# Seven products of a pair: three calls of 256 columns instead of one of 512 and one of 256, in three of fourteen pairs of a layer

## The chip, the core and the metric

One core of a Trainium2 chip runs the whole program in one launch. The metric is the device time of that launch in microseconds; the time of before is the median of three runs. One more execution was taken with the hardware profiler; all rows of the profile come from it.

## What is computed

A decoder trunk of two layers on one sequence of 512 tokens, 1024 wide, in 32-bit floats. Each layer has a mixer (windowed attention and retention behind one projection) and then an MLP with 4096 hidden columns. Only the MLP matters here:

```python
h2 = rmsnorm(x, g_mlp)
x = x + jnp.square(jax.nn.relu(h2 @ w_up)) @ w_down
```

## The kernel before

Every array lies with its features on the 128 partitions and the 512 tokens along the free dimension. To keep precision, each operand is split into a high and a low part (`hi` and `lo`); ACT copies the high part (L239), and DVE subtracts it from the value to give the low part (L240). A product of two such operands is three calls on TensorE: high by high, high by low, low by high (`products`, L284 to L286).

Weights come in units of 128 x 1024 floats. SP issues their loads (L183; for pairs L197, L199 and L202) into `raw` tiles, of which there are three; then follow the split on ACT and DVE into `hi` and `lo` tiles (three buffers each), and the calls on TensorE. `unit` takes the next unit and sees that the two behind it are being split already.

The MLP runs in the order of `mlp_sequence`. Its hidden columns are 32 chunks of 128. The first four go as one group ("first"); their results are scaled, cut at zero, squared and split by `put_up` (L1018, L1019, L291, L292). The other 28 go as 14 pairs of two neighbouring chunks, named here by the first of the two: 4, 6, 8, ... 30. Between the pairs stand the "down" steps (`two_chunks`), which multiply a quarter of the hidden columns into two chunks of the result. The two pairs 4 and 6 follow the first group directly; the last pair is 30; behind it the last quarter goes down, in layer 1 by `end`, which works on halves of 256 tokens and keeps the splits of its last five weight units in the tiles named `r`.

A pair is computed by seven products of half size instead of eight: the two chunks, the two halves of the input features and the two halves of the tokens (`H` = 256 each) make 2 x 2 blocks. The four parts of a pair (`order` entries with part 0 to 3) are weight blocks and sums of them, built on DVE (`add_part`, L208 to L216). `block` gives parts of the input, `form` sums of them (in r tiles). Each of the seven products runs over four slices of 128 features. Their accumulators are three PSUM banks, `a`, `e` and `b`; `b` starts as a copy of `a`, made by ACT (L1065), onto which TensorE goes on accumulating.

In each slice the high weights meet the high and the low part of the input in one call of 512 columns (L1041), and the low weights meet the high part in one of 256 (L1042). So each accumulator has two halves of 256 columns, and the halves have to be added afterwards: `join` (a copy of one half on ACT, L1047, and a sum on DVE, L1048), and `join_copied` (three sums on DVE, L1052 to L1054, with the copies `eu` and `bu` that ACT makes at L1067 and L1070). Then the result is scaled and cut at zero (L1085), squared (L1088) and split (L291, L292).

The order on each engine is fixed when the program is built, by a scheduler that places the instructions; engines wait for each other by semaphores. ACT, DVE and SP each work strictly through their own list. PSUM has five banks for such products (`ps_mm`).

Of the kernel before, what the change touches and what calls it, by code (L numbers as in the profile page):

```python
# [12 lines left out]
AF = mybir.ActivationFunctionType  # L13
ALU = mybir.AluOpType
# [3 lines left out]
P = 128  # L18
# [29 lines left out]
DEEP = 3  # L48
DELAY = 2
ASIDE = 48  # L50


def unit_order():
# [21 lines left out]
def mlp_sequence():  # L75

    seq = [("first", 0, 0), ("pair", 0, 2), ("pair", 0, 3)]
    for q in range(3):  # L80
        for i in range(4):
            seq += [("down", q, i), ("pair", q + 1, i)]
    return seq + [("last", 3, 0)]


class Slots:
# [29 lines left out]
def decoder(ctx, tc, xT, x_first, w_in, w_a, w_b, w_out, w_up, w_down, tables, decay, band, out):  # L116
    nc = tc.nc
    weights = {"w_in": w_in, "w_a": w_a, "w_b": w_b, "w_out": w_out, "w_up": w_up, "w_down": w_down}
# [6 lines left out]
    ps_mm = ctx.enter_context(tc.tile_pool(name="ps_mm", bufs=5, space=PSUM))  # L125
# [5 lines left out]
    def temp(name="t"):  # L131
        return tmp.tile([P, T], F32, tag="t", name=name)

    def big(name, dtype=F32):
        return tmp.tile([P, 2, T], dtype, tag="big", name=name, bufs=6)

    def bank(pool, name):
        return pool.tile([P, T], F32, tag=pool.name, name=name)
# [11 lines left out]
    xh, xl = xhl[:, 0], xhl[:, 1]  # L150
# [4 lines left out]
    order = [(layer, *u) for layer in range(DEPTH) for u in unit_order()]  # L155
# [62 lines left out]
    def split_until(n):  # L218
        while state["split"] < min(n, len(order)):
            i = state["split"]  # L220
            load_until(i + 3)
            paired = order[i][1] == "pair"
            if paired:
                add_part(i)
            raw = raws[i]
            if homes and i >= len(order) - len(homes):
                home = homes[len(order) - 1 - i]
                hi, lo = (home[:, 2 * a : 2 * a + 2, :].rearrange("p a t -> p (a t)") for a in range(2))
            else:

                first = (ASIDE, 0) if paired else (ASIDE, ASIDE) if i >= len(order) - 8 else (0, 0)
                hi, lo = (
                    wpool.tile([P, UNIT + P], F32R, tag=n, name=n)[:, a : a + UNIT] for n, a in zip(("hi", "lo"), first)
                )
            for at in (LEFT,) if paired and order[i][3] == 3 else halves(i):
                if i == 0 and at.start == 0:
                    nc.vector.tensor_copy(hi[:, at], raw[:, at])
                else:
                    nc.scalar.activation(hi[:, at], raw[:, at], AF.Copy)  # L239
                nc.vector.tensor_tensor(lo[:, at], raw[:, at], f32(hi[:, at]), ALU.subtract)  # L240
            raws.pop(i - 3 if paired else i, None)
            parts[i] = (hi, lo)
            state["split"] += 1

    def unit(name, layer):
        i = state["next"]
        assert order[i][:2] == (layer, name), (order[i], layer, name)
        state["next"] += 1
        split_until(i + 3)
        return parts.pop(i)  # L250
# [27 lines left out]
    def products(ps, pairs, start, stop, resume=False):  # L278


        n = len(pairs)
        for i, ((ah, al), (bh, bl)) in enumerate(pairs):
            more = {"skip_group_check": True} if resume else {}
            nc.tensor.matmul(ps, ah, bh, start=start and i == 0, stop=False, **more)  # L284
            nc.tensor.matmul(ps, ah, bl, start=False, stop=False, **more)  # L285
            nc.tensor.matmul(ps, al, bh, start=False, stop=stop and i == n - 1, **more)  # L286
# [197 lines left out]
    def layer_body(layer):  # L484
        g_mix, g_mlp = 2 * layer, 2 * layer + 1
        rms_mix, rms_mlp = Rms(g_mix), Rms(g_mlp)
# [410 lines left out]
        for u in range(4):  # L897
            hi, lo = unit("w_a", layer)
            for j in range(2):
                c = 2 * u + j  # L900
                ps = bank(ps_mm, "mm")
                pairs = []
# [76 lines left out]
        H = T // 2  # L979
# [26 lines left out]
        def form(j):  # L1006
            return [by_form[2 * (j // 2) + k // 2][:, j % 2, k % 2, :, :] for k in range(4)]

        def block(half, tokens):
            at = slice(tokens * H, tokens * H + H)  # L1010
            return [xhl[:, :, k, at] for k in range(4 * half, 4 * half + 4)]
# [13 lines left out]
        def up_home():  # L1025

            if any(len(f) == 4 for f in slots.free):
                t, own = slots.four()
                return t[:, 0:2, :], t[:, 2:4, :], own
            return big("uhi", F32R), big("ulo", F32R), []  # L1030

        def pair(q):
            def multiply(ps, weights, left, moving, start=True):


                hi, lo = weights
                more = {} if start else {"skip_group_check": True}
                both = ps.rearrange("p (s t) -> p s t", t=H)
                for k, m in enumerate(moving):
                    c = slice((0 if left else 4 * P) + k * P, (0 if left else 4 * P) + (k + 1) * P)  # L1040
                    nc.tensor.matmul(both, hi[:, c], m, start=start and k == 0, stop=False, **more)  # L1041
                    nc.tensor.matmul(ps[:, :H], lo[:, c], m[:, 0, :], start=False, stop=k == 3 and start, **more)  # L1042

            def join(dest, ps):

                side = temp("side")[:, :H]
                nc.scalar.activation(side, ps[:, H:], AF.Copy)  # L1047
                nc.vector.tensor_tensor(dest, ps[:, :H], side, ALU.add)  # L1048

            def join_copied(dest, ps, u):  # L1050

                nc.vector.tensor_tensor(u[:, :H], u[:, :H], u[:, H:], ALU.add)  # L1052
                nc.vector.tensor_tensor(u[:, :H], u[:, :H], ps[:, H:], ALU.add)
                nc.vector.tensor_tensor(dest, ps[:, :H], u[:, :H], ALU.add)  # L1054

            a, e, b = (bank(ps_mm, "mm") for _ in range(3))
            eu, bu, z = temp("eu"), temp("bu"), big("z")
            part = unit("pair", layer)
            multiply(a, part, True, block(0, 0))
            nc.scalar.activation(b, a, AF.Copy)  # L1065
            multiply(e, part, False, form(0))
            nc.scalar.activation(eu, e, AF.Copy)  # L1067
            part = unit("pair", layer)
            multiply(b, part, True, form(1), False)
            nc.scalar.activation(bu, b, AF.Copy)  # L1070
            multiply(a, part, False, block(1, 0), False)
            join(z[:, 0, :H], a)
            part = unit("pair", layer)
            multiply(b, part, True, form(2), False)
            join_copied(z[:, 1, H:], b, eu)
            multiply(e, part, False, block(1, 1), False)
            join_copied(z[:, 0, H:], e, bu)
            part = unit("pair", layer)
            multiply(b, part, True, form(3), False)
            for half in (1, 0):  # L1080
                at = slice(half * H, half * H + H)
                if half == 0:
                    join(z[:, 1, at], b)
                factor = rms_mlp.value[:, at].unsqueeze(1).broadcast_to([P, 2, H])
                nc.vector.scalar_tensor_tensor(z[:, :, at], z[:, :, at], 0.0, factor, ALU.max, ALU.mult)  # L1085
            hi, lo, own = up_home()
            for i in range(2):
                nc.scalar.activation(z[:, i, :], z[:, i, :], AF.Square)  # L1088
                split(hi[:, i, :], lo[:, i, :], z[:, i, :])
                up[q].append((hi[:, i, :], lo[:, i, :]))  # L1090
            up_slots[q].extend(own)
# [18 lines left out]
        for what, q, i in mlp_sequence():  # L1110
            if what == "first":
                group("w_up", layer, xs, [put_up] * 4, first_hooks())
            elif what == "pair":
                pair(q)
                if (q, i) == (3, 3):
                    for t in sums:
                        slots.give(*t[1])
            elif what == "down":
                two_chunks("w_down", layer, up[q], [put_down(2 * i), put_down(2 * i + 1)])
                if i == 3:  # L1120
                    slots.give(*up_slots[q])
            elif layer == DEPTH - 1:
                end(layer, up[q])
            else:
                group("w_down", layer, up[q], [put_down(c, True) for c in range(4)])
                for c in range(4, KD):
                    chunk("w_down", layer, up[q], put_down(c, True))
                slots.give(*up_slots[q])
# [156 lines left out]
```

## Time and profile before

| | us |
|---|---|
| median of 3 runs | 1505.27 |
| lowest and highest run | 1504.72, 1505.3 |
| profiled execution | 1504.95 |
| span of its trace | 1503.2 |
| TensorE busy in it | 1488.1 |
| DVE busy | 1076.2 |
| ACT busy | 763.3 |

In the rows shown below, PE is TensorE, PEld its loads of weights, and SPq the queue that SP issues to. A row of instructions in order of time has the start and the duration in us, the engine, the source line, the operation, the tiles (written <- read), the shape, how many there are, and in brackets how long the engine had been idle and what ended that. A tile's name is without its number, so that all `hi` tiles read alike; `mm` is an accumulator, `xhl` the split input of the layer, `r` a slot of the store for split activations and, in `end`, for weights, `uhi` and `ulo` split hidden columns outside that store. A row of a table by stretches has the stretch, its length, and each engine's busy time with the number of instructions, then the granted clock of TensorE, the share of the DMA engines and what they moved.

### The profile page before, as it was taken

The page shows a single profiled execution, that of the slowest core. Times are in us where ns is not written, and L with a number is a line of the kernel's source. Part 1 is how long each engine was busy: PE and PEld are TensorE (multiplying, and loading weights), DVE is VectorE, ACT ScalarE, POOL GpSimd, SP SyncE. Part 2 cuts the span into 40 slices and gives each one's busy share as a digit, 9 for nine tenths or more (in the row PEclk, how much of TensorE's full clock was granted, in tenths as well). Part 3 has the DMA queues.
Part 4 walks back from the last instruction along what each step waited for, and adds up shares of the span by engine and source line. Part 5 has one row for each costly group of instructions (what it writes and reads, how often), then busy time and mean ns, then how long its engine had stood idle before and what let it go on. Part 6 is the DMA issues. An engine that isn't in the chain of part 4 may idle for free.

```text
span 1503.2 us, 19211 instructions
## 1 busy us (share of the span) xinstructions
PE 1488.1 (99%) x7298; PEld 1255.5 (84%) x7298; DVE 1076.2 (72%) x1738; ACT 763.3 (51%) x1219; POOL 2.9 (0%) x13
## 2 busy tenths in 40 slices
PE   9999999999999999999999999999999999999997
PEld 7888888888888888888888888888888788888887
DVE  7877568754788777777677865777449877777774
ACT  6657355532555445545465742555326555454462
POOL 0000000000000000000000000000000000000000
PEclk9999999999999999999999999999999999999999
DMA  6422323244323333324443223222443232343331
GB/s 221 133 86 71 98 84 92 70 126 126 99 70 113 98 113 93 104 85 147 155 125 92 85 85 102 80 78 84 126 126 98 71 110 86 99 126 99 111 100 57
DMA packets 52636, 155.02 MB, mean 103 GB/s; under 512 B 6208, under 2 KB 8384, under 8 KB 52544
## 3 DMA queue, kind: packets, MB, share of 16 engines
q1 hardware_dynamic: 52400, 153.54, 33.9%
q8 instruction: 57, 0.93, 0.3%
q14 instruction: 35, 0.29, 0.1%
q10 hardware_dynamic: 144, 0.26, 0.0%
HBM read 146.96 MB, written 4.19 MB: 101 GB/s over the span
## 4 chain that ended last, share of the span: by engine, by line
PE 95%; DVE 2%; ACT 1%; DMA 1%; issue 1%; DVEq 0%
PE mm L284 22%; PE mm L285 22%; PE mm L286 22%; PE mm L1041 11%; PE mm L1042 5%; PE rv L284 2%; PE rv L286 2%; PE rv L285 2%; PE score L655 1%; PE pT L620 1%; PE r L285 1%; PE r L286 1%; PE r L284 1%; DMA raw<-w_down_in 1%; DVE lo L240 1%
## 5 line engine op out<-in xcount | busy, mean ns | idle before, releaser
L239 ACT ACTIVATE hi<-raw 128x1024 fp32r<-128x1024 f32 (+1 forms) x313 | 315.7, 1013 | 448.9 <-PE mm L285 252.6
L240 DVE TENSOR_TENSOR lo<-raw,hi 128x1024 fp32r<-128x1024 f32 (+1 forms) x314 | 363.9, 1163 | 168.8 <-ACT hi L239 168.0
L284 PE MATMUL mm<-r,hi 128*128 128x512 f32 (+1 forms) x688 | 264.3, 388 | 2.1 <-ACT hi L239 2.1
L285 PE MATMUL mm<-r,hi 128*128 128x512 f32 (+1 forms) x688 | 266.2, 387 | 0.0
L284 PE MATMUL mm<-xhl,hi 128*128 128x512 f32 x672 | 262.7, 393 | 0.0
L286 PE MATMUL mm<-r,lo 128*128 128x512 f32 (+1 forms) x688 | 262.3, 387 | 0.0
L285 PE MATMUL mm<-xhl,hi 128*128 128x512 f32 x672 | 261.7, 392 | 0.0
L286 PE MATMUL mm<-xhl,lo 128*128 128x512 f32 x672 | 260.5, 392 | 0.0
L1041 PE MATMUL mm<-r,hi 128*128 128x512 f32 x448 | 158.7, 392 | 1.9 <-ACT mm L1065 1.7
L284 PEld LDWEIGHTS mm<-r,hi 128*128 128x128 f32 x688 | 128.7, 188 | 28.5 <-ACT hi L239 2.7
L286 PEld LDWEIGHTS mm<-r,lo 128*128 128x128 f32 x688 | 129.1, 188 | 26.9
L285 PEld LDWEIGHTS mm<-r,hi 128*128 128x128 f32 x688 | 129.1, 188 | 25.4
L286 PEld LDWEIGHTS mm<-xhl,lo 128*128 128x128 f32 x672 | 126.3, 188 | 25.1
L284 PEld LDWEIGHTS mm<-xhl,hi 128*128 128x128 f32 x672 | 126.2, 188 | 24.7 <-ACT xhl L294 0.4
L285 PEld LDWEIGHTS mm<-xhl,hi 128*128 128x128 f32 x672 | 126.4, 188 | 24.3
L1042 PE MATMUL mm<-r,lo 128*128 128x256 f32 x448 | 124.4, 278 | 0.1
L1041 PE MATMUL mm<-xhl,hi 128*128 128x512 f32 x336 | 119.2, 391 | 0.1
L1041 PEld LDWEIGHTS mm<-r,hi 128*128 128x128 f32 x448 | 84.1, 188 | 20.9 <-ACT mm L1065 3.7
L1042 PE MATMUL mm<-xhl,lo 128*128 128x256 f32 x336 | 93.0, 277 | 0.0
L1042 PEld LDWEIGHTS mm<-r,lo 128*128 128x128 f32 x448 | 84.1, 188 | 2.7 <-DVE lo L240 1.0
L1041 PEld LDWEIGHTS mm<-xhl,hi 128*128 128x128 f32 x336 | 63.1, 188 | 13.7 <-ACT eu L1067 0.9
L1042 PEld LDWEIGHTS mm<-xhl,lo 128*128 128x128 f32 x336 | 63.1, 188 | 1.7
(200 smaller groups left out, 2113.6 us busy)
## 6 DMA issues: line engine op xcount, KB each, us to landing
raw<-w_in_in SPq DMA_DIRECT2D x89, 512.0 KB, 3.6
raw<-w_down_in SPq DMA_DIRECT2D x64, 512.0 KB, 3.6
raw<-w_up_in SPq DMA_DIRECT2D x36, 512.0 KB, 3.6
raw<-w_up_in SPq DMA_DIRECT2D x56, 256.0 KB, 2.7
raw<-w_b_in SPq DMA_DIRECT2D x16, 512.0 KB, 3.6
raw<-w_out_in SPq DMA_DIRECT2D x16, 512.0 KB, 3.8
raw<-w_a_in SPq DMA_DIRECT2D x8, 512.0 KB, 3.5
x<-xT_in SPq DMA_DIRECT2D x15, 256.0 KB, 3.9
```

The costliest lines, as they stand in the source:

```text
L239: nc.scalar.activation(hi[:, at], raw[:, at], AF.Copy)
L240: nc.vector.tensor_tensor(lo[:, at], raw[:, at], f32(hi[:, at]), ALU.subtract)
L284: nc.tensor.matmul(ps, ah, bh, start=start and i == 0, stop=False, **more)
L285: nc.tensor.matmul(ps, ah, bl, start=False, stop=False, **more)
L286: nc.tensor.matmul(ps, al, bh, start=False, stop=stop and i == n - 1, **more)
L620: nc.tensor.transpose(pt[:, i * P : (i + 1) * P], sm[:, at : at + P], ident)
L655: nc.tensor.matmul(ps[:, g * w : (g + 1) * w], q_s[g][:, c, at], part[:, keys], start=i == 0, stop=i == 1)
L1041: nc.tensor.matmul(both, hi[:, c], m, start=start and k == 0, stop=False, **more)
L1042: nc.tensor.matmul(ps[:, :H], lo[:, c], m[:, 0, :], start=False, stop=k == 3 and start, **more)
```

## The change

Eleven of the fourteen pairs of a layer (8 to 28) keep the calls of 512 and 256 columns. Pairs 4, 6 and 30 take `narrow_pair`: each slice of each product is three calls of 256 columns (`products`), all into one accumulator of 256 columns. With that the halves vanish, and with them `join`, `join_copied` and the copy `bu`; the copies of `a` to `b` and of `e` and `b` to `eu` have 256 columns. DVE reads the accumulators directly: two sums, two scalings of 256 columns and one of 2 x 256.

Three things go with it. The low parts of the weights of the three pairs lie 48 floats into their tile, as the high parts do (`ASIDE`); in the other pairs they stay at its start. The banks are taken in the order b, a, e instead of a, e, b, in all pairs. And the first pair with 512 columns in a layer (pair 8) makes one more call of 512 columns into `b` before ACT copies `a` there; its result is overwritten by that copy.

The diff, cut to its core (`join`, `join_copied` and the inside of the old multiply are unchanged):

```diff
+FIRST_WIDE, LAST_WIDE = 8, 30
+def wide(chunk):
+    return FIRST_WIDE <= chunk < LAST_WIDE
...
-                first = (ASIDE, 0) if paired else (ASIDE, ASIDE) if i >= len(order) - 8 else (0, 0)
+                first = (ASIDE, ASIDE) if paired or i >= len(order) - 8 else (0, 0)
+                if paired and wide(order[i][2]):
+                    first = (ASIDE, 0)
...
+        def narrow_pair():
+            def multiply(ps, weights, left, moving, start=True):
+                hi, lo = weights
+                cols = [slice((0 if left else 4 * P) + k * P, (0 if left else 4 * P) + (k + 1) * P) for k in range(4)]
+                pairs = [((hi[:, c], lo[:, c]), (m[:, 0, :], m[:, 1, :])) for c, m in zip(cols, moving)]
+                products(ps, pairs, start, True, not start)
+            b, a, e = (bank(ps_mm, "mm")[:, :H] for _ in range(3))
+            eu, z = temp("eu"), big("z")
+            part = unit("pair", layer)
+            multiply(a, part, True, block(0, 0))
+            nc.scalar.activation(b, a, AF.Copy)
+            multiply(e, part, False, form(0))
+            nc.scalar.activation(eu[:, :H], e, AF.Copy)
+            part = unit("pair", layer)
+            multiply(b, part, True, form(1), False)
+            nc.scalar.activation(eu[:, H:], b, AF.Copy)
+            multiply(a, part, False, block(1, 0), False)
+            nc.vector.scalar_tensor_tensor(z[:, 0, :H], a, 0.0, rms_mlp.value[:, :H], ALU.max, ALU.mult)
+            part = unit("pair", layer)
+            multiply(b, part, True, form(2), False)
+            nc.vector.tensor_tensor(z[:, 1, H:], b, eu[:, :H], ALU.add)
+            multiply(e, part, False, block(1, 1), False)
+            nc.vector.tensor_tensor(z[:, 0, H:], e, eu[:, H:], ALU.add)
+            part = unit("pair", layer)
+            multiply(b, part, True, form(3), False)
+            later = rms_mlp.value[:, H:].unsqueeze(1).broadcast_to([P, 2, H])
+            nc.vector.scalar_tensor_tensor(z[:, :, H:], z[:, :, H:], 0.0, later, ALU.max, ALU.mult)
+            nc.vector.scalar_tensor_tensor(z[:, 1, :H], b, 0.0, rms_mlp.value[:, :H], ALU.max, ALU.mult)
+            return z
...
-        def pair(q):
+        def wide_pair(first):
...
-            a, e, b = (bank(ps_mm, "mm") for _ in range(3))
+            b, a, e = (bank(ps_mm, "mm") for _ in range(3))
             part = unit("pair", layer)
             multiply(a, part, True, block(0, 0))
+            if first:
+                nc.tensor.matmul(b, part[0][:, :P], xh[:, 0, :], start=True, stop=True)
             nc.scalar.activation(b, a, AF.Copy)
...
+        def pair(q, i):
+            c = 8 * q + 2 * i
+            z = wide_pair(c == FIRST_WIDE) if wide(c) else narrow_pair()
             hi, lo, own = up_home()
```

More of the change, by code (lines that the diff above doesn't have):

```diff
@@ L1085, in pair @@
                 nc.vector.scalar_tensor_tensor(z[:, :, at], z[:, :, at], 0.0, factor, ALU.max, ALU.mult)
+            return z
+        def pair(q, i):
+            c = 8 * q + 2 * i
+            z = wide_pair(c == FIRST_WIDE) if wide(c) else narrow_pair()
             hi, lo, own = up_home()
@@ L1113, in layer_body @@
             elif what == "pair":
-                pair(q)
+                pair(q, i)
                 if (q, i) == (3, 3):
```

## The prediction, as it was put on record

> **What bounds the kernel now.** I read the page's summary first, then the chain that ended last, then a table by stretches, then TensorE (PE) in order of time where that table shows idle time.
>
> ```profile
> span 1503.2 us, 19211 instructions
> ...
> PE 1488.1 (99%) x7298; PEld 1255.5 (84%) x7298; DVE 1076.2 (72%) x1738; ACT 763.3 (51%) x1219; POOL 2.9 (0%) x13
> ...
> PE 95%; DVE 2%; ACT 1%; DMA 1%; issue 1%; DVEq 0%
> ```
>
> TensorE is the bound: 95% of the last chain. A change can gain by fewer or faster products, or where PE stands still. The stretches around the edited pairs:
>
> ```profile
> 433.40:470.00 36.60, 34.62 (x183) 28.64 (x182) 29.57 (x48) 23.93 (x40) 0.00 (x0) 1.00 0.30 94
> 1174.50:1212.00 37.50, 35.38 (x186) 29.28 (x185) 30.21 (x49) 24.66 (x41) 0.00 (x0) 1.00 0.31 92
> 690.00:716.00 26.00, 26.00 (x129) 21.99 (x129) 18.39 (x28) 13.48 (x21) 0.96 (x1) 1.00 0.44 142
> 1446.70:1470.06 23.36, 22.58 (x185) 21.88 (x184) 14.67 (x24) 14.47 (x26) 0.00 (x0) 1.00 0.30 94
> ```
>
> The columns are length, then busy time of PE, weight loads, DVE (VectorE) and ACT (ScalarE). PE idles 1.98 us around the first two pairs of layer 0 and 2.12 us around those of layer 1, nothing around the last pair of layer 0, and 0.78 us in the stretch right behind the last pair of layer 1. The clock is 1.00 in all four, so no stretch is slow by its clock. Inside the first stretch PE's starts say where:
>
> ```profile
> 436.54 0.28 PE L1042 MATMUL mm<-r,lo 128*128 128x256 f32 x1
> 437.68 0.50 PE L1041 MATMUL mm<-r,hi 128*128 128x512 f32 x1 [0.86 <-ACT mm L1065]
> 438.01 0.28 PE L1042 MATMUL mm<-r,lo 128*128 128x256 f32 x1
> ...
> 446.19 0.40 PE L1041 MATMUL mm<-xhl,hi 128*128 128x512 f32 x1
> 446.64 0.38 PE L1042 MATMUL mm<-r,lo 128*128 128x256 f32 x1
> 446.87 0.40 PE L1041 MATMUL mm<-r,hi 128*128 128x512 f32 x1
> ...
> 450.32 0.28 PE L1042 MATMUL mm<-r,lo 128*128 128x256 f32 x1
> 451.63 0.50 PE L284 MATMUL mm<-r,hi 128*128 128x512 f32 x1 [1.03 <-ACT hi L239]
> 451.97 0.40 PE L285 MATMUL mm<-r,hi 128*128 128x512 f32 x1
> 452.39 0.50 PE L1041 MATMUL mm<-xhl,hi 128*128 128x512 f32 x1
> ...
> 467.00 0.28 PE L1042 MATMUL mm<-r,lo 128*128 128x256 f32 x1
> 467.26 0.50 PE L1041 MATMUL mm<-r,hi 128*128 128x512 f32 x1
> ```
>
> Products overlap, so their price is the distance between starts, not the listed duration. The next rows give it: two ends of an even run each, in the order wide pair, 256-column products undisturbed, the same after a stop, and 256-column products with weights from the end's r tiles.
>
> ```profile
> 439.16 0.39 PE L1041 MATMUL mm<-xhl,hi 128*128 128x512 f32 x1
> 444.94 0.39 PE L1041 MATMUL mm<-r,hi 128*128 128x512 f32 x1
> ...
> 1448.73 0.28 PE L284 MATMUL mm<-uhi,hi 128*128 128x256 f32 x1
> 1450.89 0.28 PE L285 MATMUL mm<-ulo,hi 128*128 128x256 f32 x1
> ...
> 1473.04 0.28 PE L284 MATMUL mm<-uhi,hi 128*128 128x256 f32 x1
> 1475.40 0.28 PE L286 MATMUL mm<-uhi,lo 128*128 128x256 f32 x1
> ...
> 1462.56 0.28 PE L284 MATMUL mm<-r,r 128*128 128x256 f32 x1
> 1468.92 0.28 PE L286 MATMUL mm<-r,r 128*128 128x256 f32 x1
> ```
>
> Wide: 5.78 us for 17 couples of 512 and 256 columns, 0.340 each (0.227 and 0.113). Narrow: 2.16 us for 19 products, 0.1137; after a stop 2.36 for 20, 0.118; with the r tiles 6.36 for 53, 0.120.
>
> Against these distances the stops of layer 0 are: at 437 1.14 - 0.11 = 1.03, and 0.10 more on the next product (0.33 instead of 0.227); at 446 0.22 + 0.12; at 451 1.20 + 0.11; at 452 0.19, and at 467 0.15, each with about 0.11 on the product behind it. Sum **3.34 us**. Layer 1 idles 0.14 more in its stretch (2.12 against 1.98): 3.48.
>
> **The change part by part.** *Products.* A wide pair is 28 couples, 28 x 0.340 = 9.52 us; a narrow one is 84 products, 84 x 0.1137 = 9.55. So in an undisturbed stream the edit costs PE 0.03 per pair, 0.09 per layer: the columns are the same, only the loads of weights are more. That price is not shown for these operands; I take the 0.1137 of weights that lie with the same offset as the new ones, and bound it by 0.113 (the share in a wide couple) and 0.120 (the r tiles). For the 84 x 6 = 504 narrow products that is nothing at one end and 504 x 0.0063 = 3.2 us at the other.
>
> Against this part stands a rule. Each product brings its own load, and the rows of loads say:
>
> ```profile
> L1042 PEld LDWEIGHTS mm<-r,lo 128*128 128x128 f32 x448 | 84.1, 188 | 2.7 <-DVE lo L240 1.0
> ...
> 1449.42 0.19 PEld L285 LDWEIGHTS mm<-ulo,hi 128*128 128x128 f32 x1
> ```
>
> The load at 1449.42 begins 0.11 before its product starts, beside the product ahead of it. The Trainium skill (page "TensorE: Matmul & The Clock Gate", Part 3, "The mechanism") says that a load runs beside a product in flight only where their row groups differ; these all take the full 128 rows. By that page's section "LDWEIGHTS (loading the stationary operand)", 128 columns over 1.2 GHz, an estimate of 107 ns, the 168 more loads would cost 18 us. The trace disagrees with the rule: 0.1137 per product leaves no room for a load in the open. It stays a rival below, priced by rows.
>
> *Stops at the first two pairs.* Three rows of ACT:
>
> ```profile
> 437.05 0.57 ACT L1065 ACTIVATE mm<-mm 128x512 f32<-128x512 f32 x1
> ...
> 441.57 0.36 ACT L1047 ACTIVATE side<-mm 128x256 f32<-128x256 f32 x1
> ...
> 450.52 1.06 ACT L239 ACTIVATE hi<-raw 128x1024 fp32r<-128x1024 f32 x1 [0.73 <-PE mm L1041]
> ```
>
> The stop at 437 is the copy of a into b. It begins only at 437.05, though a was long complete, because ACT first squares and splits the four results of the "first" group. The built order of the new kernel leaves that queue as it is, so this stop **stays**; the copy of 256 columns takes 0.36 instead of 0.57, and the stop shrinks from 1.13 to 0.92. At 446 PE waits for a lo part behind four DVE operations of the two pairs; three remain. Between 0 and 0.34; I take the middle, 0.17. The stop at 451 is a buffer: the hi tile of the first down unit is free only when pair 4's fourth part has been multiplied (450.52 starts as that ends), and PE has nothing left to do during the 1.06 of the split. In the new order that fourth part is multiplied before most of pair 6, and 24 narrow products (2.7 us) stand between the release of the down unit's buffer and its first use: the 1.31 goes. The 0.30 at 452 and the 0.26 at 467 are copies on ACT (L1067, L1065) that stood behind a late split and late squares; with the joins gone, both have 2.7 us of products ahead of their use: 0. What would be late next there is the lo part of pair 6's first unit, with some 0.1 us in hand; that is inside the range.
>
> *Added.* One product of 512 columns in each layer's first wide pair, 0.23. And what remains of pairs 4 and 6 behind the stop that stays, 60 + 84 products, probably runs at 0.118: 144 x 0.0043 = 0.62 (between 0, if the even spacing returns at once, and 144 x 0.0063 = 0.91).
>
> Per layer: 0.92 + 0.17 + 0.23 + 0.62 + 0.09 = 2.03 in the place of 3.34 and 3.48: 1.31 + 1.45 = **2.76 gained**. The other pairs keep their work; that b is now the first of the three banks changes which earlier reader must be done, and PE's even stream there gives me no wait to charge. The built order also moves loads on SP's queue:
>
> ```profile
> raw<-w_up_in SPq DMA_DIRECT2D x56, 256.0 KB, 2.7
> ```
>
> In pair 8 this load (raw2) goes out ahead of the third load of its pair instead of behind it, in pair 10 behind the first. The others wait for a raw buffer anyway, so I take nothing; at worst the sums that need it come 2.7 us later.
>
> *Last pair.* In layer 0 PE has no idle time to give back (26.00 of 26.00). In layer 1 the end follows:
>
> ```profile
> 1455.41 0.86 PE L284 MATMUL mm<-r,r 128*128 128x256 f32 x5
> 1456.76 0.39 PE L285 MATMUL mm<-r,r 128*128 128x256 f32 x1 [0.48 <-DVE r L292]
> ...
> 1459.74 0.28 PE L286 MATMUL mm<-r,r 128*128 128x256 f32 x1
> 1460.31 0.39 PE L284 MATMUL mm<-r,r 128*128 128x256 f32 x1 [0.29 <-DVE x L430]
> ```
>
> Five products take 1.35 instead of 0.60, and the second stop is 0.57 instead of 0.12; with 0.1 behind each, 1.40. The first waits for the split of this very pair's result, the second for DVE, which comes late from the last weights. On DVE:
>
> ```profile
> 1451.40 0.69 DVE L1085 SCALAR_TENSOR_TENSOR z<-z,rstd 128x512 f32<-128x512 f32 x1
> 1452.00 1.22 DVE L240 TENSOR_TENSOR r<-raw,r 128x1024 fp32r<-128x1024 f32 x1
> ```
>
> The join and this scaling (about 1 us together) stand ahead of a weight split whose raw buffer the next load needs. Without them split, load and the last lo parts come about 0.9 earlier, and in the new order the banks' readers no longer stand behind the last split. Bounds: 0, if the landing of the loads sets the end, and 1.40; nearest to the row on DVE I take **1.2**.
>
> Sum: 2.76 + 1.2 = 3.96. The profiled execution took 1504.95, 1.75 more than its span; the median of the runs is 1505.27, 0.32 above it. From the median: **1501.3 us**.
>
> **The rivals.**
> 1. *The narrow stream runs at 0.120*, as with the r tiles: 216 products that I took at 0.1137 and 288 at 0.118 cost 1.4 + 0.6 more: 1503.2. For it: two spacings above 0.1137 stand in the trace. Against: all products with weights from the same pool and offset start at 0.1137 until something stops them.
> 2. *The end gives nothing*: the last loads land when they do now. 1502.5. For it: the second stop hangs on a load; against: that load's issue waits for DVE.
> 3. *The loads don't hide*, the slower one. Place: pairs 4, 6 and 30. Each of 28 more loads per pair stands in the open with its 188 ns: 168 x 0.188 = 31.6, 1532.9. It takes back the whole gain from (3.96 + 1.24) / 504 = 0.0103 over 0.1137, 0.124 per product, and is slower by 3 us from 0.130. No 256-column stream above is over 0.120. It is what the rule of the Trainium skill ("TensorE: Matmul & The Clock Gate", Part 3) would make of the edit.
> 4. *The edit doesn't remove what it seems to*: the 451 stop stays because the down unit's split is late for another reason: 2 x 1.31 less gain, 1503.9.
>
> **How the numbers follow.** A measurement of this kernel can tell about 0.2% from no change, here 3.0 us, so faster means below 1502.3. The forecast with its own spread (1499.5, with no slow spacing, no stop at 446 and all of the end, to 1502.3) has 0.66; rival 1 0.14, rival 2 0.10, rival 3 0.05, rival 4 0.05. Faster: 0.66 and a little of rival 2, 0.68; same: rivals 1, 4 and most of 2, 0.27; slower 0.05. The range takes in rivals 1, 2 and 4 at its upper end, and at its lower the 1499.5 less the 0.6 by which the three runs of before differ: 1498.9 to 1503.9.
>
> **What would show it.** In the changed profile: 256-column products of the narrow pairs 0.113 to 0.118 apart (rival 1: 0.120; rival 3: over 0.124); one stop of 0.9 us in pair 4, in front of the first product into b, released by the 256-column copy; no wait of the first down chunk for hi; and less than 0.4 us lost behind the last pair of layer 1. A new stop of over 0.5 us in pairs 4 to 8, or in the wide pairs by their new bank order, would make the prediction wrong.

## The result, and the profile after

| | before | after |
|---|---|---|
| median, us | 1505.18 | 1500.74 |
| lowest and highest run, us | 1504.72, 1505.33 | 1500.29, 1501.05 |
| runs | 8 | 8 |
| profiled execution, us | 1504.95 | 1500.69 |
| span of its trace, us | 1503.2 | 1498.8 |

The changed kernel takes 4.44 us less: a ratio of 0.9971, interval 0.996 to 0.9981. The forecast was 1501.3, 0.56 above. In the changed kernel the same helper lines stand some ten lines lower: `products` is L293 to L295, the split of weights L248 and L249, that of activations L300 and L301, the scaling and squaring L1027 and L1028, the sums into `x` at the end L439 (L430 before), the calls of a wide pair L1085 and L1086, the copy of `a` to `b` in a narrow pair L1056, in a wide pair L1111.

First the summary and the last line of the chain of waits:

```profile
span 1498.8 us, 19490 instructions
...
PE 1487.5 (99%) x7468; PEld 1265.3 (84%) x7468; DVE 1066.0 (71%) x1708; ACT 757.9 (51%) x1207; POOL 2.9 (0%) x13
...
PE 99%; ACT 1%; DVE 0%; issue 0%; DVEq 0%
```

TensorE is busy as long as before (1487.5 against 1488.1), with 170 more products. What went is its waiting: its share of the chain rises from 95% to 99%. The table by stretches, laid as before from just ahead of pair 4 in each layer, says where:

```profile
433.85:470.45 36.60, 36.03 (x246) 33.31 (x245) 27.35 (x40) 22.15 (x36) 0.00 (x0) 1.00 0.28 87
1173.33:1210.83 37.50, 36.93 (x250) 34.08 (x249) 28.25 (x41) 22.95 (x37) 0.00 (x0) 1.00 0.27 85
690.00:716.00 26.00, 26.00 (x157) 23.21 (x156) 15.94 (x21) 12.30 (x18) 0.96 (x1) 1.00 0.43 142
1444.64:1465.70 21.06, 21.06 (x179) 21.06 (x178) 12.98 (x21) 13.29 (x23) 0.00 (x0) 1.00 0.27 95
```

PE's idle time around the first two pairs falls from 1.98 and 2.12 us to 0.57 in each layer, and behind the last pair of layer 1 from 0.78 to nothing. The clock is 1.00 as before. In order of time, TensorE in pairs 4 and 6 of layer 0:

```profile
434.37 0.28 PE L293 MATMUL mm<-xhl,hi 128*128 128x256 f32 x1
...
437.08 0.28 PE L295 MATMUL mm<-r,lo 128*128 128x256 f32 x1
437.92 0.39 PE L293 MATMUL mm<-r,hi 128*128 128x256 f32 x1 [0.57 <-ACT mm L1056]
438.15 0.28 PE L294 MATMUL mm<-r,hi 128*128 128x256 f32 x1
...
443.92 0.34 PE L295 MATMUL mm<-xhl,lo 128*128 128x256 f32 x1
444.10 0.28 PE L293 MATMUL mm<-xhl,hi 128*128 128x256 f32 x1
...
453.52 0.28 PE L295 MATMUL mm<-r,lo 128*128 128x256 f32 x1
453.63 0.40 PE L293 MATMUL mm<-r,hi 128*128 128x512 f32 x1
```

Read the distances between starts. From 434.37 to 437.08 stand 23 of them, from 438.15 to 443.92 49, from 444.10 to 453.63 81: 0.1178 each time. One stop is left, 437.08 to 437.92; with the longer distance behind it, it costs 0.72 + 0.11. Around 443.92 a wait of 0.06 is left. The first down product, at 453.63, follows 0.11 behind the last narrow one: the stop of 1.31 is gone. ACT shows why the one stayed and the other went:

```profile
436.99 0.61 ACT L1028 ACTIVATE up<-up 128x512 f32<-128x512 f32 x1
437.50 0.36 ACT L1056 ACTIVATE mm<-mm 128x256 f32<-128x256 f32 x1
...
450.89 1.06 ACT L248 ACTIVATE hi<-raw 128x1024 fp32r<-128x1024 f32 x1 [0.67 <-PE mm L294]
```

The copy of `a` into `b` comes only when ACT has done the squares of the first group. The split for the down unit now starts at 450.89, 2.7 us ahead of its first use. No new stop stands in the wide pairs: in pair 24 both kernels lose about 0.15 and 0.11 in each layer, and no other wait there is over 0.05. Three anchors put the gain in its places; first two rows of before, then one of after (the start of pair 4 in the second layer), then one more (the end of the end's stretch):

```profile
433.92 0.40 PE L1041 MATMUL mm<-xhl,hi 128*128 128x512 f32 x1
...
1175.21 0.40 PE L1041 MATMUL mm<-xhl,hi 128*128 128x512 f32 x1
```

```profile
1174.04 0.28 PE L293 MATMUL mm<-xhl,hi 128*128 128x256 f32 x1
...
1465.70 0.59 PE L452 MATMUL ssq<-acc,ones 128*128 128x256 f32 x2
```

From pair 4 of one layer to pair 4 of the next: 741.29 before, 739.67 after, **1.62 gained in layer 0**. The end's stretch is 23.36 before and 21.06 after, but six of its products (0.71) now run ahead of it: **1.59 gained at the end**. From pair 4 of layer 1 to the start of that stretch, 271.48 and 270.60, and the same 0.71 to be added: **1.59 in layer 1**. Together 4.80; pair 4 of layer 0 began 0.45 later in this execution (starts of 433.7 to 434.8 occur in kernels that are alike up to there), which leaves the 4.4 between the spans.

What changed at the end stands in DVE's list. Two rows of before, then two of after:

```profile
1456.02 1.29 DVE L292 TENSOR_TENSOR r<-z,r 128x512 fp32r<-128x512 f32 x2
1459.84 1.74 DVE L430 TENSOR_TENSOR x<-x,mm 128x256 f32<-128x256 f32 x5
```

```profile
1449.53 0.68 DVE L301 TENSOR_TENSOR r<-z,r 128x512 fp32r<-128x512 f32 x1
1454.81 1.08 DVE L439 TENSOR_TENSOR x<-x,mm 128x256 f32<-128x256 f32 x3
```

Counted from the start of the stretch, with the 0.71 taken into account, the split of the last pair's result is at least 3.7 us earlier and the first sums into `x` 2.3 earlier. In the kernel before those sums stood behind the last weight split (1458.70); now they stand ahead of it (1455.80). The three weight splits ahead of that one start 0.85, 0.69 and 0.80 earlier.

### The profile page after: what moved, and what is told of

The parts are those of the page before. It is cut to its first block, busy times and chain, and to the rows that moved or that the text cites. A ratio compares the mean times of both kernels' runs of the same rounds, so it can differ in the third digit from the quotient of the medians.

```text
span 1498.8 us, 19490 instructions
## 1 busy us (share of the span) xinstructions
PE 1487.5 (99%) x7468; PEld 1265.3 (84%) x7468; DVE 1066.0 (71%) x1708; ACT 757.9 (51%) x1207; POOL 2.9 (0%) x13
## 4 chain that ended last, share of the span: by engine, by line
PE 99%; ACT 1%; DVE 0%; issue 0%; DVEq 0%
PE mm L293 24%; PE mm L295 24%; PE mm L294 24%; PE mm L1085 9%; PE mm L1086 5%; PE rv L293 2%; PE rv L294 2%; PE rv L295 2%; PE score L664 1%; PE pT L629 1%; PE r L294 1%; PE r L295 1%; PE r L293 1%; PE pv L649 0%; PE pv L650 0%; PE ssq L387 0%
## 5 line engine op out<-in xcount | busy, mean ns | idle before, releaser
L248 ACT ACTIVATE hi<-raw 128x1024 fp32r<-128x1024 f32 (+1 forms) x313 | 315.2, 1013 | 451.7 <-PE mm L294 278.6
L249 DVE TENSOR_TENSOR lo<-raw,hi 128x1024 fp32r<-128x1024 f32 (+1 forms) x314 | 363.8, 1164 | 166.7 <-ACT hi L248 165.6
L294 PE MATMUL mm<-r,hi 128*128 128x512 f32 (+1 forms) x784 | 292.9, 374 | 0.0
L293 PE MATMUL mm<-r,hi 128*128 128x512 f32 (+1 forms) x784 | 291.6, 375 | 1.1 <-ACT mm L1056 1.1
L295 PE MATMUL mm<-r,lo 128*128 128x512 f32 (+1 forms) x784 | 288.4, 374 | 0.0
L293 PE MATMUL mm<-xhl,hi 128*128 128x512 f32 (+1 forms) x744 | 283.1, 383 | 0.0
L294 PE MATMUL mm<-xhl,hi 128*128 128x512 f32 (+1 forms) x744 | 281.8, 381 | 0.0
L295 PE MATMUL mm<-xhl,lo 128*128 128x512 f32 (+1 forms) x744 | 280.8, 381 | 0.0
L293 PEld LDWEIGHTS mm<-r,hi 128*128 128x128 f32 x784 | 146.8, 188 | 27.4 <-ACT mm L1056 1.5
L295 PEld LDWEIGHTS mm<-r,lo 128*128 128x128 f32 x784 | 147.0, 188 | 26.6
L293 PEld LDWEIGHTS mm<-xhl,hi 128*128 128x128 f32 x744 | 140.2, 189 | 24.8 <-ACT xhl L303 0.4
L295 PEld LDWEIGHTS mm<-xhl,lo 128*128 128x128 f32 x744 | 139.8, 188 | 25.0
L1085 PE MATMUL mm<-r,hi 128*128 128x512 f32 x352 | 124.4, 391 | 0.0
L1086 PE MATMUL mm<-r,lo 128*128 128x256 f32 x352 | 97.5, 277 | 0.0
L1085 PE MATMUL mm<-xhl,hi 128*128 128x512 f32 x264 | 93.3, 390 | 0.0
L1085 PEld LDWEIGHTS mm<-r,hi 128*128 128x128 f32 x352 | 66.1, 188 | 14.2 <-ACT mm L1111 0.6
L1086 PE MATMUL mm<-xhl,lo 128*128 128x256 f32 x264 | 73.1, 277 | 0.0
L1086 PEld LDWEIGHTS mm<-r,lo 128*128 128x128 f32 x352 | 66.1, 188 | 1.7
L1146 DVE TENSOR_TENSOR x<-x,mm 128x512 f32<-128x512 f32 x56 | 37.8, 686 | 39.0 <-PE mm L295 39.0
L1085 PEld LDWEIGHTS mm<-xhl,hi 128*128 128x128 f32 x264 | 49.6, 188 | 10.2
```

The source lines that it names most:

```text
L1146: nc.vector.tensor_tensor(x[:, c, :], x[:, c, :], ps, ALU.add)
```

## The experiments

Each ran beside the kernel before on one chip; "less" is against its median in the same batch: 1504.92 for the first four, 1504.97 for the next four, 1505.22 for the last.

### The first two pairs alone, the last pair alone, none, all

The theory: three separate sums (stops at the first pairs, stops at the end, a small price per narrow pair). The rivals: the new order of the banks, which is the same in the first three of these runs, brings the gain, or the last pair gives nothing.

```diff
-FIRST_WIDE, LAST_WIDE = 8, 30
+FIRST_WIDE, LAST_WIDE = 8, 32     # first two alone
+FIRST_WIDE, LAST_WIDE = 4, 30     # last alone
+FIRST_WIDE, LAST_WIDE = 4, 32     # no narrow pair
+FIRST_WIDE, LAST_WIDE = 0, 0      # all narrow
```

> Only pairs 4 and 6 narrow, pair 30 wide. My theory (the gain of the first two pairs is the stops that vanish there, the gain of pair 30 is the stops of the end behind it): per layer 3.5 us of stops become 0.9, the added call costs 0.23, and 168 narrow products at the 0.1178 seen in the changed kernel cost 0.75 more: 1.6 gained per layer, 3.2 in all, 1502.0 us; the end keeps its two stops. Rival (the new order of the banks brings the gain): 1500.7, as with pair 30, since the order of the banks is the same.

Measured 1501.84, 3.08 less, ratio 0.9978 (0.997 to 0.9987). The stops of the end are still in this trace:

```profile
1452.11 0.76 PE L293 MATMUL mm<-r,r 128*128 128x256 f32 x5
1453.28 0.39 PE L294 MATMUL mm<-r,r 128*128 128x256 f32 x1 [0.42 <-DVE r L301]
...
1457.14 0.39 PE L293 MATMUL mm<-r,r 128*128 128x256 f32 x1 [0.61 <-DVE x L439]
```

They are the two that the prediction quotes, with the same releasers. So the first two pairs bring their 3.1 alone, and the end needs the last pair.

> Only pair 30 narrow, pairs 4 and 6 wide (the added call now in pair 4). My theory: the end's stops go, about 1.7 us, against 0.37 for each of the two narrow pairs and 0.46 for the two added calls: 0.5 gained, 1504.7 us; all stops of the first two pairs are there. Rival (pair 30 gives nothing, the loads of the end decide): 1506.4, and the two stops of the end remain.

Measured 1504.09, 0.83 less, ratio 0.9996 (0.9987 to 1.0005): by itself this can't be told from no change. Its trace has neither of the two stops at the end (one wait of 0.22 is left, at 1452), and the stops of the first pairs stand, the first one shorter (0.62 idle, against 0.86), as the added product now runs ahead of it, and the one at 446 too (0.06 against 0.22). With the run ahead of it the parts make 3.91 of 4.44.

> All fourteen pairs wide, with the new order of the banks and the added call in pair 4. My theory: no stop goes, except that the first shrinks by the time of the added call, which PE spends ahead of it: 1505.2 us within 0.3. Rival (the order of the banks brings a part of the gain): 1501 to 1504.

Measured 1504.83, ratio 0.9999 (0.999 to 1.0008). The new order of the banks gives nothing that can be told from no change. The added product costs nothing here, where TensorE waits anyway: the idle time in front of the copy's reader falls from 0.86 to 0.63. One thing was unexpected, the distance behind the stop:

```profile
437.78 0.50 PE L1085 MATMUL mm<-r,hi 128*128 128x512 f32 x1 [0.63 <-ACT mm L1111]
438.12 0.28 PE L1086 MATMUL mm<-r,lo 128*128 128x256 f32 x1
...
445.82 0.28 PE L1086 MATMUL mm<-r,lo 128*128 128x256 f32 x1
```

22 couples in 7.70 us, 0.350 each, where the kernel before needs 0.340 for the same pair.

> All fourteen pairs narrow, no added call. If 0.1178 is the spacing of every stream of such products: 28 narrow pairs cost 28 x 0.37 = 10.4 us, against 5.2 for the stops of the first pairs, 1.7 for the end and 0.5 for the stop in pair 20: 1508.2 us. If the slow spacing comes only behind a stop, as I had it in the prediction, most pairs run at 0.1137 and cost nothing: 1499 us.

Measured 1505.26, 0.34 more, ratio 1.0003 (0.9994 to 1.0012). Ten periods of one pair and the down steps beside it in the kernel before, then nine in this one, by the table of stretches:

```profile
497.31:702.99 205.68, 205.68 (x1042) 174.77 (x1041) 158.18 (x241) 101.28 (x151) 0.96 (x1) 1.00 0.34 103
```

```profile
507.77:694.87 187.10, 187.10 (x1190) 170.09 (x1189) 126.19 (x172) 83.40 (x118) 0.00 (x0) 1.00 0.28 99
```

20.57 against 20.79, without idle time in either (the stop that the text above places in pair 20 is that of pair 24, in layer 0 at 631 us of the kernel before, and is gone here): a narrow pair is 0.22 dearer, not 0.03, and not the 0.37 of 84 x 0.1178 against 28 x 0.340. Counted by starts, the wide pairs of this stretch take about 9.6 each, not 9.52, and the narrow ones 9.9; the rest of the difference lies among the down products and is not resolved. With all 28 pairs narrow, their price is about what the vanished stops bring; with three per layer it is not. In the same trace stands a stretch that runs otherwise, first in layer 0, then its counterpart in layer 1:

```profile
438.50 0.28 PE L294 MATMUL mm<-r,hi 128*128 128x256 f32 x1
...
443.94 0.28 PE L294 MATMUL mm<-xhl,hi 128*128 128x256 f32 x1
...
1180.42 0.28 PE L294 MATMUL mm<-r,hi 128*128 128x256 f32 x1
...
1186.19 0.34 PE L295 MATMUL mm<-xhl,lo 128*128 128x256 f32 x1
```

In layer 0 these are 48 distances of 0.1133, at the place (pair 4, behind its stop) where the changed kernel runs the same calls at 0.1178. In layer 1 of this very run the same calls, behind the same stop, are 0.1178 apart (49 distances), and so are the other stretches of pairs 4 and 6 in both layers.

### The stop that stayed: the copy on DVE

The theory: `b` is late because of ACT's queue alone. The rival: the copy comes late whoever makes it.

```diff
-            nc.scalar.activation(b, a, AF.Copy)
+            if early:                       # in pair 4
+                nc.vector.tensor_copy(b, a)
+            else:
+                nc.scalar.activation(b, a, AF.Copy)
```

> The changed kernel, but in pair 4 DVE makes the copy of a into b, not ACT. My theory (the stop that stays, 0.84 us per layer in the changed kernel, is ACT's queue of squares and splits): the stop goes in both layers, 1.7 us less than the changed kernel, 1499.0 us. Rival (the copy is late whoever makes it, as DVE is as full there): 1500.7, with the stop now released by DVE.

Measured 1498.83 (1498.02 to 1499.42), 6.14 less, ratio 0.9958 (0.9946 to 0.9971). The copy on DVE, then TensorE:

```profile
436.37 0.43 DVE L1057 COPY mm<-mm 128x256 f32<-128x256 f32 x1
```

```profile
434.75 0.28 PE L293 MATMUL mm<-xhl,hi 128*128 128x256 f32 x1
...
443.47 0.34 PE L295 MATMUL mm<-xhl,lo 128*128 128x256 f32 x1
```

74 distances in 8.72 us, 0.1178 each: no stop, and none over 0.07 behind it in pairs 4 and 6 of either layer. The theory holds: from pair 4 to the end of the span (1497.6) the run needs 1062.85 us, 1.58 less than the 1064.43 of the changed kernel, where two stops of 0.83 stood.

### The added product

The theory: in pair 8 nothing waits that the 512 columns could hide behind.

```diff
-            if first:
-                nc.tensor.matmul(b, part[0][:, :P], xh[:, 0, :], start=True, stop=True)
```

> The changed kernel without the added call of 512 columns in pair 8. If it costs its 0.227 us on PE in each layer: 1500.3 us. If it fills time in which PE would wait for the copy into b anyway: 1500.7.

Measured 1499.52, 5.45 less, ratio 0.9964 (0.9952 to 0.9977). Against the kernel before beside each, that is 1.0 more than the changed kernel gained, but part of it lies ahead of the change:

```profile
433.84 0.28 PE L293 MATMUL mm<-xhl,hi 128*128 128x256 f32 x1
```

From there to the end of the span (1497.8) are 1063.96 us, against the same 1064.43: 0.47, two products of 0.23.

### The place of the weights in their tiles

Is 0.1178 a matter of where the weights lie in their tile? With the offset at 0, and at 32 floats, instead of 48:

```diff
-                first = (ASIDE, ASIDE) if paired or i >= len(order) - 8 else (0, 0)
+                first = (0, 0) if paired else (ASIDE, ASIDE) if i >= len(order) - 8 else (0, 0)
```

(the second run has `(32, 32)` in place of `(0, 0)` for the pairs)

> The changed kernel, but the weights of the three narrow pairs start at 0 in both tiles instead of 48 floats into them. If the place of the weights sets the spacing, as the 0.120 of the r tiles suggested: 504 products x 0.0022 more than the 0.1178 seen, 1501.8 us. If it doesn't: 0.1178 and 1500.7.

> The same with an offset of 32 floats in both tiles. If 48 is not the best place, the spacing falls under 0.1178, to 0.1137 at best, 2.1 us less: 1498.6. If the place doesn't matter beyond the first step: 0.1178, 1500.7.

Measured 1500.96, ratio 0.9974 (0.9963 to 0.9984), and 1501.2, ratio 0.9975 (0.9965 to 0.9985). With offset 0, 44 distances from the first to the second of these rows:

```profile
439.76 0.28 PE L293 MATMUL mm<-xhl,hi 128*128 128x256 f32 x1
...
445.04 0.28 PE L295 MATMUL mm<-xhl,lo 128*128 128x256 f32 x1
```

0.120 each, the price of rival 1. With 32 floats the 80 distances from 443.67 to 453.27 are 0.120 too, the 49 from 437.70 to 443.51 0.1186; no stretch is under 0.1178, so a better place was not found. The other narrow stretches that I read, in pairs 4, 6 and 30, are 0.1196 to 0.1199 apart with 0, 0.1186 to 0.1204 with 32, and 0.1176 to 0.1179 in the changed kernel. So the distance goes with the place. The two medians can't be told from that of the changed kernel, but from pair 4 to the end of the span these traces need 0.75 and 0.94 more than its 1064.43, where 504 x 0.0022 would be 1.1.

### Both edits together

```diff
-            nc.scalar.activation(b, a, AF.Copy)          # pair 4: nc.vector.tensor_copy(b, a)
...
-            if first:
-                nc.tensor.matmul(b, part[0][:, :P], xh[:, 0, :], start=True, stop=True)
```

> The changed kernel with both edits that gained alone: the copy of a into b in pair 4 made by DVE instead of ACT, and pair 8 without the added product of 512 columns. My theory: the first removes a wait of TensorE behind ACT's queue (0.84 us per layer), the second 0.23 us of work per layer, and they lie in different pairs, so they add up: about 1498.4, no stop in pair 4 and all pairs up to the first down chunk in one even stream. Rival: the copy made by DVE has used up the slack of the low parts, so that the missing product only lets TensorE come to a low part earlier and wait for it: 1498.8, with a stop of about 0.2 in pair 6 or behind pair 8.

Measured 1498.63 (1498.47 to 1498.81), 6.59 less, ratio **0.9957** (0.9945 to 0.997). It is faster than both kernels: all five runs lie below all eight of the changed one, whose lowest is 1.66 above the median here; the kernel before had the same median beside both (1505.18 and 1505.22). Span and first product of pair 4:

```profile
span 1496.7 us, 19484 instructions
```

```profile
434.18 0.28 PE L293 MATMUL mm<-xhl,hi 128*128 128x256 f32 x1
```

1062.52 from pair 4 on, 1.91 under the changed kernel's 1064.43; the one edit had 1.58 and the other 0.47. They add up within 0.15, and no stop of the 0.2 that the rival named stands in pair 6 or 8 (0.07 is the longest). Against the run with DVE's copy alone the times themselves show no difference.

### How many of the first pairs must be narrow

```diff
-FIRST_WIDE, LAST_WIDE = 8, 30
+FIRST_WIDE, LAST_WIDE = 6, 30     # on top of both edits
```

> The kernel of the run before it, with pair 6 in calls of 512 and 256 columns again, so that pairs 4 and 30 alone are narrow. My theory: a narrow pair costs 0.245 us on TensorE and the stops that went hung on the whole of pairs 4 and 6 as the joins crowd ACT and DVE, so pair 6 in wide form gives back some of them: the hi of the first down unit is waited for again, up to 1.3 us per layer, 1498.4 - 0.5 + 2.6 = 1500.5 at most, 1499.2 if half of it comes back. Rival: all that stood in the way was the copy of a into b and the order of pair 4; then pair 6 wide only saves its 0.245 per layer: 1497.9.

Measured 1499.3 (1498.28 to 1499.71), ratio 0.9961 (0.9948 to 0.9973). ACT's split for the first down unit, then TensorE: the product ahead of the down unit and the first of the down unit, then a stop in pair 8, and one at the end:

```profile
449.22 1.06 ACT L248 ACTIVATE hi<-raw 128x1024 fp32r<-128x1024 f32 x1
```

```profile
451.74 0.28 PE L1089 MATMUL mm<-r,lo 128*128 128x256 f32 x1
451.86 0.40 PE L293 MATMUL mm<-r,hi 128*128 128x512 f32 x1
...
464.06 0.28 PE L1089 MATMUL mm<-r,lo 128*128 128x256 f32 x1
464.34 0.50 PE L1088 MATMUL mm<-r,hi 128*128 128x512 f32 x1
...
1453.24 0.28 PE L295 MATMUL mm<-r,r 128*128 128x256 f32 x1
1454.15 0.36 PE L293 MATMUL mm<-r,r 128*128 128x256 f32 x1 [0.63 <-DVE x L439]
```

The split waits for nothing, and the down unit follows 0.12 behind. My theory, that both pairs are needed for this, falls; pair 4 alone takes the stop away. That 1499.3 lies beside the 1499.2 of my theory is luck, as the wait that should have come back did not. The 0.49 that a wide pair 6 should save shows in no time, for other stops are there. At 464 stands the one that the kernel before had at 467 (0.16 and 0.11, the same in layer 1); with pair 6 narrow it is gone. And this trace has a stop of 0.8 at the end, which hung on DVE; why it came is not shown. From pair 4 (433.74) to the end of the span (1497.0) this trace needs 1063.26, 0.74 more than with pair 6 narrow. By the times, whether pair 6 is better wide or narrow stays open: the intervals lie over each other.

### DVE's copy without any narrow pair

```diff
-FIRST_WIDE, LAST_WIDE = 8, 30
+FIRST_WIDE, LAST_WIDE = 4, 32
...
-            if first:
-                nc.tensor.matmul(b, part[0][:, :P], xh[:, 0, :], start=True, stop=True)
-            nc.scalar.activation(b, a, AF.Copy)
+            if first:
+                nc.vector.tensor_copy(b, a)
+            else:
+                nc.scalar.activation(b, a, AF.Copy)
```

> No narrow pair at all and no added product; only the new order of the banks and, in pair 4, the copy of a into b (512 columns) made by DVE. My theory: the copy is one stop of several, the stops at the low part of pair 4's last unit and at the hi of the first down unit have causes of their own and stay or grow a little: the first stop of about 0.9 goes in both layers, and a part of it comes back as a longer wait behind it: 1503.2. Rival: the later stops end at times that ACT and the loads set, so that they grow by all that the first gave: 1504.8. Second rival: the first stop is the cause of all of them, and the narrow pairs gain nothing of their own: 1498.5.

Measured 1502.91, 2.31 less, ratio 0.9987 (0.9978 to 0.9995), near the 1503.2 of the theory. The copy's stop is gone. The wait for a low part at 446 has grown from 0.22 to 0.33 (the text above calls it the low part of pair 4's last unit; it is that of pair 6's second), and the one at the down unit stands as in the kernel before:

```profile
449.75 0.28 PE L1086 MATMUL mm<-r,lo 128*128 128x256 f32 x1
451.06 0.50 PE L293 MATMUL mm<-r,hi 128*128 128x512 f32 x1 [1.03 <-ACT hi L248]
```

```profile
449.95 1.06 ACT L248 ACTIVATE hi<-raw 128x1024 fp32r<-128x1024 f32 x1 [0.73 <-PE mm L1085]
```

ACT stands idle for 0.73 until TensorE is done with pair 4's last part, which here comes as late as in the kernel before. With the run above, both follow: the two stops have causes of their own, and only the narrow form of pair 4, with the order that goes with it, takes the second away.

### A lead of couples ahead of the last pair

The theory was that 256-column products run at 0.1133 when something slower ahead of them gives their loads a lead.

```diff
+            for _ in range(4 if lead else 0):      # pair 30, into the whole bank of b
+                nc.tensor.matmul(full, part[0][:, :P], xh[:, 0, :], start=True, stop=True)
+                nc.tensor.matmul(b, part[1][:, :P], xh[:, 0, :H], start=True, stop=True)
```

> The changed kernel with four couples of a 512 and a 256 column product ahead of the first product of pair 30 in both layers, into the bank of b; ACT's copy overwrites them. They add 4 x 0.340 = 1.36 us per layer. My theory (the distance of 256 column products depends on what runs ahead of them, and couples give a lead): the 84 products of pair 30 then start 0.1133 apart instead of 0.1178: 1500.7 + 2.7 - 0.75 = 1502.7. Rival (the operands and their places set the distance, whatever runs ahead): 0.1178 again, 1503.4. The rows of TensorE decide, more than the time.

Measured 1503.4, ratio 0.9989 (0.998 to 0.9998). The first couple, the first narrow product, and the down product that follows 72 of the 84 narrow ones:

```profile
692.55 0.39 PE L1057 MATMUL mm<-xhl,hi 128*128 128x512 f32 x1
...
693.95 0.28 PE L293 MATMUL mm<-xhl,hi 128*128 128x256 f32 x1
...
702.43 0.40 PE L293 MATMUL mm<-r,hi 128*128 128x512 f32 x1
```

Four couples take 1.40, 0.350 each, and the 72 distances up to 702.43 are again 0.1178. The theory falls; the rival's time was met.

## Why the prediction was right

- **The stop that stays**: predicted 0.92, 0.83 left. Its cause, ACT's queue, is shown by the copy on DVE.
- **The stop at the down unit** (1.31): predicted gone, and gone. That the released buffer decides is shown from both sides by the runs with pair 6 wide and with no narrow pair.
- **The stops at 452 and 467**: predicted 0, found 0. **The lo part at 446** (pair 6's second unit): predicted 0.17, found 0. The 0.06 that is left around 443.92 is a wait for the low part of pair 6's first unit, which DVE writes from 442.60 to 443.82; the prediction had named it as next, with 0.1 in hand, and charged nothing.
- **The added product**: predicted 0.23 per layer, measured 0.47 for both.
- **The narrow products**: the sum was right by luck, its working was not. I charged 0.03 per pair undisturbed and 0.62 per layer for products "after a stop", 1.42 in all. The changed kernel runs at 0.1178 from the first product, ahead of any stop, and in pair 30 without one. But wide pairs were dearer too than the 0.340 that I read in one stretch (about 0.343 a couple over ten pairs). The net price, 0.22 by the run with all pairs narrow, makes 1.3 for six pairs.
- **Layers 0 and 1**: predicted 1.31 and 1.45, measured 1.62 and 1.59. Of the differences, 0.31 and 0.14, the copy's stop and the low parts explain 0.19 in each layer; what is left, 0.12 and -0.05, I have not followed.
- **The end**: predicted 1.2 with a ceiling of 1.40, measured 1.59. The mechanism held: the weight splits came 0.7 to 0.85 earlier ("about 0.9" was forecast) and the readers of the banks no longer stand behind the last split. The ceiling was too low: I had counted two stops, and smaller ones of 0.07 to 0.12, ahead of the first (at 1451, 1453 and 1455 us), went too.
- **The total**: the three places gained 0.84 more than forecast, the end the most of it (0.39). The later start of pair 4 hides 0.45 of that in the spans, so that the total came out only 0.5 over the forecast's 3.96.

In the narrow pairs, rival 1's distance of 0.120 appeared only with the weights moved to 0 or 32 floats. Rivals 2 and 4 are refuted by the end's stretch and the down unit. Rival 3, loads in the open, would have shown over 0.124 per product. The loads of the changed kernel, by groups of instructions:

```profile
L294 PEld LDWEIGHTS mm<-r,hi 128*128 128x128 f32 x784 | 147.2, 188 | 25.4
```

Each takes 188 ns, yet a product with its load passes every 118 ns, so loads and products must overlap. The Trainium skill ("TensorE: Matmul & The Clock Gate", Part 3, "The mechanism") says that a load overlaps with products in flight only where the row groups differ; this trace, with full 128 rows throughout, disagrees with that sentence. The same section also has a load pulled ahead when it goes to the background weight buffer, an exception that the prediction left out; the trace agrees with an overlap, but doesn't show by which way it comes about.

## What to carry to other kernels

When the bounding engine is busy 99% of the time, list its few stops and find for each the queue or buffer behind it: here one stood behind squares in ACT's list, one behind a buffer that the order of the work held too long, one behind late splits and sums on DVE, and each went with a different part of the edits. A form that costs the bounding engine a little more work pays where it takes a stop away and loses everywhere else: three pairs of fourteen gained 4.4 us, all fourteen nothing that could be measured. Ask first whether the late operation can go to another engine; moving one copy in each layer was worth 1.6 us more.

## What the hardware showed that was not expected

The same 256-column calls with new weights run at two distances. In pair 4 behind the stop it is 0.1178 in the changed kernel, and in the one with all pairs narrow 0.1133 in layer 0 but 0.1178 in layer 1. Couples of 512 and 256 columns take 0.340 in pair 4 of the kernel before, 0.350 there with none narrow, and 0.340 again with none narrow and DVE's copy. With the weights 0 or 32 floats into their tiles instead of 48 the 256-column calls are mostly 0.120 apart. A stop alone doesn't choose between 0.1133 and 0.1178 (0.1178 stands ahead of the first one, and behind the same stop in layer 1), nor do couples ahead, nor the places: as the two programs are built, the calls of this stretch in layer 0 use the same banks and the same addresses in both. What does choose is not settled. At 0.0045 a call, the 504 narrow products hold 2.3 us of it.
